# A one-layer hybrid decoder step: four weight halves and most parameters issued by GpSimd instead of SP and ACT

## Chip, cores and metric

One core of a Trainium2 chip runs the whole step in one launch. The metric is the device time of one execution in microseconds; the profile is of another execution, taken by the hardware profiler. Times in the rows count from the start of the profiled span.

## What is computed

1024 prompt tokens and 64 sample tokens (8 sequences of 8) go through one layer; everything is float32.

```
h    = rms_norm(x, norm_g)
proj = h @ w_in                       # (tokens, 1024) x (1024, 3088)
a, gl, zc, q, k, v, zg, lr = split(proj)
u    = a * sigmoid(gl)                # 512 channels
cv   = depthwise_causal_conv(u, width 31)
cv   = silu(group_layer_norm(cv)) @ w_pw + b_pw
cv   = cv * silu(zc)
gk   = log_sigmoid(lr @ w_alpha + b_alpha) / 16
o, S = gla_chunked(q, k, v, gk, S0)   # gated linear attention, 4 heads
o    = per_head_rms_norm(o) * gla_g * silu(zg)
y    = rms_norm(x + concat(cv, o) @ w_out, final_g)
```

The outputs are y, the last 30 rows of u and the states S, for prompt and samples apart. The parameters that are vectors (norm_g, conv_w, biases, and so on) come in one array `par` of 128 x 152; columns 0 to 7 hold norm_g, the last one the epsilon of the norms.

## The kernel before

Every float32 matmul operand is split in two float32r parts, hi and lo (ACT copies hi, VectorE subtracts to get lo), and three float32r matmuls stand for one float32 product: hi x hi, hi x lo and lo x hi. A weight tile of 128 output channels comes in two halves of 4 x 128 rows of w_in (256 KB each): `s_gl0_1` is the staged second half of tile 0 of gl, `h_gl0_1` and `l_gl0_1` its parts.

Tokens go in three blocks (`CHUNKS`): number 0 (0 to 383), number 1 (384 to 767) and number 2 (768 to 1087, with the samples). Number 2 is loaded and used first (`FIRST = 2`), and for the first four weight tiles (gl0, a0, gl1, a1) it is multiplied before its norm is known: `raw_split` scales x by norm_g alone (`hh`, `hl`), and the factor rs comes in afterwards. Blocks 0 and 1 are normed first: `rms_scale` squares the eight x tiles on ACT (`sq0_k`, `sq1_k`), adds them on VectorE, sums over channels on TensorE (`ms`) and takes Ln and Exp on ACT (`rs`); `rms_split` scales x on VectorE and splits it into `hh` and `hl`.

Operations are recorded in program order by `prog.add` with a cost, and `Program.schedule` then lists them: on each engine it takes, at the planner's own time, the ready operation with the lowest priority number. Loads on SP and ACT share one planned data path (`dma_end`); operations on POOL have a cost and a lag instead, and `o.bytes` does not count there. `prog.hold` adds a dependency for the planner. The engines then run their lists in order, and the framework puts in the semaphores that the data and the reused buffers need. Each of SP's loads also waits until the one eight places before it has landed. The buffers `wst` for staged weights are four (`NST`), and from `STAGE` on halves of the first tiles are staged in `big` buffers instead.

In the loading loop (L1047 to L1063) `par` is loaded by ACT, the first halves (`h == 0`) in two pieces each and the second halves (`h == 1`) in one, all by SP, between the x tiles of block 2.

Of the kernel before, what the change touches and what calls it, by code (L numbers as in the profile page):

```python
# [29 lines left out]
C_NG, C_BA, C_CW, C_CB, C_CG, C_CBT, C_BP, C_GG, C_EPS, NPAR = 0, 8, 10, 134, 138, 142, 146, 150, 151, 152  # L30
# [16 lines left out]
STATES_AT = 1  # L47
CN_LAST = 2
ADD_LAG = 5000
STICK = 60  # L50
SLACK = 500
SLACK_FROM = 45000
# [85 lines left out]
class Program:  # L138
# [51 lines left out]
    def schedule(self):  # L190
# [51 lines left out]
        while events:  # L242
# [18 lines left out]

            if same is not None and t > SLACK_FROM and same.prio < best.prio + STICK:
                best = same
# [72 lines left out]
def build(tc, A, O):  # L336
    nc = tc.nc
    ctx = ExitStack()
    V, S, G, T = nc.vector, nc.scalar, nc.gpsimd, nc.tensor
    prog = Program({"big": NBIG, "unit": NUNIT, "wst": NST, "wl": NW, "wh": NW, "ps": 8, "kT": 2, "S": 8, "ss": 9},  # L340
                   {"ps": 3, "unit": 8, "big": 2})
# [4 lines left out]
    def R(v):  # L346
        return v.ap() if isinstance(v, View) else v
# [50 lines left out]
    def dma(out, in_, late=False, eng="SP", small=False):  # L398
        v = out if isinstance(out, View) else in_
        if late:  # L400
            prog.hold = late
        q = nc.sync if eng == "SP" else S
        prog.add(eng, lambda: q.dma_start(R(out), R(in_)), [out], [in_], 0,  # L403
                 nbytes=v.n * 4 * (v.part[1] - v.part[0]) * (6 if small else 1))

    def dma_add(out, in_):

        prog.add("POOL", lambda: G.dma_start(R(out), R(in_), accum_op=ALU.add), [out], [in_], 1000,
                 nbytes=out.n * 4 * P, lag=ADD_LAG)

# [15 lines left out]
    with ctx:  # L426
# [9 lines left out]
        def VT(pool, tag, shape, dt, name):  # L436
            return View.of(Tile_(pool, tag, shape, dt, name))
# [14 lines left out]
        par = VT(fixed, "par", [P, NPAR], F32, "par")  # L452
# [36 lines left out]
        def x_load(c, ks=range(KT), late=False, eng="SP"):  # L489
            t0, n = CHUNKS[c]  # L490
            for k in ks:
                xk = rows("x", k, F32)[:, t0:t0 + n]
                dma(xk, A["xT"][:, k, t0:t0 + n], late, eng)
                xs[(c, k)] = xk
# [15 lines left out]
        def raw_split(ks):  # L510

            for k in ks:
                g, xk = pc(C_NG + k), xs[(FIRST, k)]
                hi, lo = part("hh", k, FIRST), part("hl", k, FIRST)
                act(hi, xk, AF.Copy, scale=g)
                stt(lo, xk, g, hi.bitcast(F32), ALU.mult, ALU.subtract)
                raw[k] = hi, lo

        def rms_scale(c):
            n = CHUNKS[c][1]  # L520
            ms = pt(f"ms{c}")[:, :n]
            g = SQ_SUM[c]
            for k in range(KT):
                sq = un(f"sq{c}_{k}")[:, :n]
                act(sq, xs[(c, k)], AF.Square)
                if k % g == 0:
                    acc = sq
                else:
                    tt(acc, acc, sq, ALU.add)
                if k % g == g - 1:  # L530
                    mm(ms, one_d, acc, k == g - 1, k == KT - 1)
            rs[c] = un(f"rs{c}")[:, :n]
            act(rs[c], ms, AF.Ln, bias=eps)
            act(rs[c], rs[c], AF.Exp, scale=-0.5)
# [11 lines left out]
        def load_split(name, src, k, m, stage=None):  # L546
            st = VT(stage or wst, "big" if stage else "wst", [P, k, m], F32, f"s_{name}")
            hi = VT(wh, "wh", [P, k, m], F32R, f"h_{name}")
            lo = VT(wl, "wl", [P, k, m], F32R, f"l_{name}")
            dma(st, src)  # L550
            split(hi, lo, st)
            return hi, lo
# [6 lines left out]
        def whalf_parts(kind, i, h, stage=None):  # L559

            name, src = f"{kind}{i}_{h}", A["w_in"][mt[(kind, i)]]
            st = VT(stage or wst, "big" if stage else "wst", [P, 4, P], F32, f"s_{name}")
            hi = VT(wh, "wh", [P, 4, P], F32R, f"h_{name}")
            lo = VT(wl, "wl", [P, 4, P], F32R, f"l_{name}")

            def piece(a, b, eng):
                dma(st[:, a:b, :], src[:, 4 * h + a:4 * h + b, :], eng=eng)
                split(hi[:, a:b, :], lo[:, a:b, :], st[:, a:b, :])

            return (hi, lo), piece  # L570
# [473 lines left out]
                mix_samples(4 + i, o[:, 256:n])  # L1044


        dma(par, A["par"], eng="ACT")  # L1047
        w0, w1 = [[], []], [[], []]
        for h in range(2):
            parts_ = []  # L1050
            for w, kind, ct in ((w0[0], "gl", 0), (w0[1], "a", 0), (w1[0], "gl", 1), (w1[1], "a", 1)):
                tiles, piece = whalf_parts(kind, ct, h, big if 4 * h + len(parts_) >= STAGE else None)
                w.append(tiles)
                parts_.append(piece)

            n = 2 if h == 0 else 4
            for j in range(0, 4, n):
                for i, piece in enumerate(parts_):
                    if i < n:
                        k = 4 * h + j + i  # L1060
                        x_load(FIRST, range(k, k + 1))
                        raw_split(range(k, k + 1))
                    piece(j, j + n, "SP")  # L1063
        rms_scale(FIRST)
        x_load(0)
        x_load(1, late=True)
# [450 lines left out]
```

## Time and profile before

| | us |
|---|---|
| median of 3 runs | 463.41 (463.18 to 463.77) |
| profiled execution | 463.69 |
| its span | 461.9 |
| TensorE busy in the span | 451.9 |
| VectorE busy | 393.1 |
| ACT busy | 306.6 |
| GpSimd busy | 19.1 |

The span is the time from the first to the last instruction that the profiler saw; the rest of the execution lies around it. Matmuls are pipelined, so the busy time of one (0.31 us for 320 columns) is longer than the distance to the next. DMA share is the mean busy share of the 16 DMA engines; a landing time is counted from the start of the issue.

### The profile page before, as it was taken

Reading aid. Unit: us, or ns where it says so; the run is one execution under the profiler, and the core shown is the slowest. Engines: PE = TensorE matmul, PEld = TensorE weight load, DVE = VectorE, ACT = ScalarE, POOL = GpSimd, SP = SyncE. Lnnn points to the kernel's source line nnn. Section 1 sums busy time; section 2 is a strip of 40 time slices with the busy share of each in tenths; the row PEclk is TensorE's granted clock in tenths of the full one; section 3 lists DMA queues with packets and bytes.
Section 4 is the critical chain, followed back from the end, with each engine's and each line's share of the span. In section 5 each row is a group of like instructions: output and inputs, shape, how many; then the busy total and the mean of one; then the engine's idle time right before and its main releaser. Section 6 shows DMA issues by size and latency. Waiting matters only on the chain.

```text
span 461.9 us, 7604 instructions
## 1 busy us (share of the span) xinstructions
PE 451.9 (98%) x2728; PEld 413.8 (90%) x2728; DVE 393.1 (85%) x629; ACT 306.6 (66%) x782; POOL 19.1 (4%) x38
## 2 busy tenths in 40 slices
PE   8899999999999999999999999999999999999994
PEld 8699989999888899898999899999999988888783
DVE  5789999999999999999999899953549847988684
ACT  7767979363643623658866797653899548879554
POOL 1000000000000000000000000000000023220000
PEclk9999999999999999999999999999999999999998
DMA  7935340141200040003211211011235474476744
GB/s 214 328 126 104 67 146 15 47 68 35 57 0 1 23 153 9 2 8 107 70 57 48 82 58 45 26 66 64 77 81 183 118 196 68 78 166 152 270 151 182
DMA packets 36485, 43.26 MB, mean 94 GB/s; under 512 B 13024, under 2 KB 21344, under 8 KB 36448
## 3 DMA queue, kind: packets, MB, share of 16 engines
q1 hardware_dynamic: 33856, 38.25, 26.5%
q0 software_dynamic: 2304, 4.20, 5.7%
q8 instruction: 21, 0.34, 0.3%
q10 hardware_dynamic: 288, 0.34, 0.2%
q14 instruction: 16, 0.13, 0.1%
HBM read 36.58 MB, written 6.19 MB: 93 GB/s over the span
## 4 chain that ended last, share of the span: by engine, by line
PE 91%; DMA 3%; ACT 2%; DVE 1%; SPq 1%; issue 1%
PE ya L415 11%; PE p_zc L415 10%; PE p_zg L415 10%; PE pv L415 10%; PE p_gl L415 9%; PE p_a L415 9%; PE p_k L415 5%; PE pw L415 5%; PE p_q L415 5%; PE yc L415 5%; PE po L415 2%; DMA x<-in_xT 2%; PE pys L415 2%; DMA s_a<-in_w_in 1%; SPq L403 1%; PE px L415 1%
## 5 line engine op out<-in xcount | busy, mean ns | idle before, releaser
L364 DVE SCALAR_TENSOR_TENSOR cv<-u,par,cv 128x1024 f32<-128x1024 f32 x120 | 150.9, 1278 | 0.2
L415 PE MATMUL p_gl<-hh,h_gl 128*128 128x384 f32 (+1 forms) x96 | 32.2, 336 | 2.0 <-ACT h_gl L358 1.3
L358 ACT ACTIVATE pr<-us,par 128x64 f32<-128x64 f32 x124 | 32.3, 343 | 0.0
L415 PE MATMUL p_gl<-hh,l_gl 128*128 128x384 f32 (+1 forms) x96 | 32.3, 336 | 0.0
L415 PE MATMUL p_gl<-hl,h_gl 128*128 128x384 f32 (+1 forms) x96 | 31.7, 331 | 0.2 <-DVE hl L364 0.2
L415 PE MATMUL p_zc<-hh,h_zc 128*128 128x384 f32 (+1 forms) x96 | 31.7, 330 | 0.0
L415 PE MATMUL p_a<-hl,h_a 128*128 128x384 f32 (+1 forms) x96 | 31.6, 329 | 0.0
L415 PE MATMUL p_zc<-hl,h_zc 128*128 128x384 f32 (+1 forms) x96 | 31.5, 328 | 0.0
L415 PE MATMUL p_zc<-hh,l_zc 128*128 128x384 f32 (+1 forms) x96 | 31.5, 328 | 0.0
L415 PE MATMUL p_zg<-hl,h_zg 128*128 128x384 f32 (+1 forms) x96 | 31.5, 328 | 0.0
L415 PE MATMUL p_zg<-hh,l_zg 128*128 128x384 f32 (+1 forms) x96 | 31.4, 327 | 0.0
L415 PE MATMUL p_zg<-hh,h_zg 128*128 128x384 f32 (+1 forms) x96 | 31.4, 327 | 0.0
L415 PE MATMUL p_a<-hh,h_a 128*128 128x384 f32 (+1 forms) x96 | 31.3, 326 | 0.0
L415 PE MATMUL p_a<-hh,l_a 128*128 128x384 f32 (+1 forms) x96 | 31.2, 326 | 0.0
L415 PE MATMUL pv<-h_v,hl 128*128 128x512 f32 x64 | 25.0, 390 | 0.0
L415 PE MATMUL pv<-l_v,hh 128*128 128x512 f32 x64 | 24.9, 390 | 0.0
L415 PE MATMUL pv<-h_v,hh 128*128 128x512 f32 x64 | 24.9, 389 | 0.0
L415 PEld LDWEIGHTS p_gl<-hh,h_gl 128*128 128x128 f32 x96 | 18.0, 188 | 3.6 <-ACT h_gl L358 2.1
L415 PEld LDWEIGHTS p_gl<-hh,l_gl 128*128 128x128 f32 x96 | 18.0, 188 | 1.3 <-DVE l_gl L368 0.4
L415 PEld LDWEIGHTS p_gl<-hl,h_gl 128*128 128x128 f32 x96 | 18.0, 188 | 0.7 <-DVE hl L364 0.4
L368 DVE TENSOR_TENSOR o<-o,zg 128x384 f32<-128x384 f32 (+1 forms) x12 | 6.2, 534 | 14.5 <-ACT zg L358 14.5
L415 PEld LDWEIGHTS p_zc<-hh,h_zc 128*128 128x128 f32 x96 | 18.1, 188 | 0.3 <-issue 0.2
(345 smaller groups left out, 1284.2 us busy)
## 6 DMA issues: line engine op xcount, KB each, us to landing
xr<-in_x SPq DMA_DIRECT2D x16, 256.0 KB, 4.8
out_y<-xr SPq DMA_DIRECT2D x15, 256.0 KB, 2.1
x<-in_xT SPq DMA_DIRECT2D x16, 192.0 KB, 5.3
T<-in_w_out POOLq DMA_DIRECT2D x12, 256.0 KB, 5.1
s_v<-in_wv SPq DMA_DIRECT2D x16, 128.0 KB, 2.8
s_zc<-in_w_in SPq DMA_DIRECT2D x8, 256.0 KB, 2.6
s_zg<-in_w_in SPq DMA_DIRECT2D x8, 256.0 KB, 2.6
s_gl<-in_w_in SPq DMA_DIRECT2D x6, 256.0 KB, 4.8
```

The lines of the kernel that those rows point to most:

```text
L358: return S.activation(R(out), R(in_), func, **kw)
L364: return prog.add("DVE", lambda: V.scalar_tensor_tensor(R(out), R(a), R(s), R(b), op0, op1), [out], [a, s, b], out.n / 0.96 + 67 + 62 * is ...
L368: return prog.add("DVE", lambda: V.tensor_tensor(R(out), R(a), R(b), op), [out], [a, b], out.n / 0.96 + 67)
L403: prog.add(eng, lambda: q.dma_start(R(out), R(in_)), [out], [in_], 0, nbytes=v.n * 4 * (v.part[1] - v.part[0]) * (6 if small else 1))
L415: o = prog.add("PE", lambda: T.matmul(R(ps), R(lhsT), R(rhs), start=start, stop=stop, skip_group_check=True), [ps], [lhsT, rhs], c / share ...
```

## The change

`dma` gets a third way of issuing: by GpSimd, with a planned cost of 1000 ns and a lag of 3500. The parameters are loaded in two pieces, columns 0 to 7 by ACT as before, the other 144 by GpSimd; the four second halves of the first four weight tiles go to GpSimd too. Each of the five is held, in the planner, behind the split of the second x tile.

```
+LOAD_LAG = 3500
@@ def dma
         q = nc.sync if eng == "SP" else S
+        if eng == "POOL":
+            prog.add(eng, lambda: G.dma_start(R(out), R(in_)), [out], [in_], 1000,
+                     nbytes=v.n * 4 * (v.part[1] - v.part[0]), lag=LOAD_LAG)
+            return
         prog.add(eng, lambda: q.dma_start(R(out), R(in_)), [out], [in_], 0,
@@ loading loop
-        dma(par, A["par"], eng="ACT")
+        dma(par[:, 0:C_BA], A["par"][:, 0:C_BA], eng="ACT")
...
                         x_load(FIRST, range(k, k + 1))
                         raw_split(range(k, k + 1))
-                    piece(j, j + n, "SP")
+                        if k == 1:
+                            started = prog.ops[-1]
+                            prog.hold = started
+                            dma(par[:, C_BA:], A["par"][:, C_BA:], eng="POOL")
+                    if h == 1:
+                        prog.hold = started
+                    piece(j, j + n, "POOL" if h == 1 else "SP")
```

The planner makes new lists for all engines. On SP before, from the fourth x tile of block 2 on; x4 to x7 of 128x320 are block 2, those of 128x384 block 0:

```order
L403 DMA x4_156<-in_xT 128x320
L403 DMA x5_167<-in_xT 128x320
L403 DMA x6_176<-in_xT 128x320
L403 DMA s_gl1_1_185<-in_w_in 128x512
L403 DMA x7_192<-in_xT 128x320
L403 DMA s_a1_1_201<-in_w_in 128x512
L403 DMA s_gl0_1_211<-in_w_in 128x512
L403 DMA x0_88<-in_xT 128x384
L403 DMA x1_98<-in_xT 128x384
L403 DMA s_a0_1_234<-in_w_in 128x512
```

And GpSimd's list with the change, from the last of its first memsets:

```order
L394 MEMSET vs_103 64x512
L405 DMA par_86<-in_par 128x144
L405 DMA s_gl1_1_168<-in_w_in 128x512
L405 DMA s_a1_1_191<-in_w_in 128x512
L405 DMA s_gl0_1_212<-in_w_in 128x512
L405 DMA s_a0_1_231<-in_w_in 128x512
L394 MEMSET u1_323 128x30
```

The four second halves have left SP's list, where x4 to x7 and the tiles of block 0 now follow each other, and stand on GpSimd behind the rest of the parameters.

ACT's list before, from the last squares of block 0 (`sq0_k`) to the first split of block 0 (`hh` of 128x384); `sq1_k` are the squares of block 1, `rs0` is the factor of block 0:

```order
L358 ACTIVATE sq0_7_363<-x7_192 128x384
L358 ACTIVATE rs0_380<-ms0_338,par_86 128x384
L358 ACTIVATE rs0_380<-rs0_380 128x384
L358 ACTIVATE sq1_0_390<-x0_88 128x384
L358 ACTIVATE sq1_1_397<-x1_98 128x384
L358 ACTIVATE hh0_114<-x0_88 128x384
L358 ACTIVATE sq1_2_407<-x2_116 128x384
L358 ACTIVATE hh1_130<-x1_98 128x384
L358 ACTIVATE hh2_172<-x2_116 128x384
L358 ACTIVATE sq1_3_423<-x3_127 128x384
```

The same place with the change:

```order
L359 ACTIVATE sq0_7_360<-x7_189 128x384
L359 ACTIVATE sq1_0_366<-x0_88 128x384
L359 ACTIVATE sq1_1_372<-x1_98 128x384
L359 ACTIVATE sq1_2_378<-x2_116 128x384
L359 ACTIVATE rs0_382<-ms0_344,par_86 128x384
L359 ACTIVATE sq1_3_389<-x3_129 128x384
L359 ACTIVATE rs0_382<-rs0_382 128x384
L359 ACTIVATE sq1_4_401<-x4_161 128x384
L359 ACTIVATE sq1_5_407<-x5_173 128x384
L359 ACTIVATE sq1_6_413<-x6_180 128x384
L359 ACTIVATE sq1_7_418<-x7_189 128x384
L359 ACTIVATE hh0_113<-x0_88 128x384
```

Two squares of block 1 stood ahead of the first split of block 0; now all eight do, three of them ahead of `rs0` as well.

TensorE's list before, at the end of block 2 (`p_a1_2`) and the start of block 0 (`p_gl0_0`):

```order
L415 MATMUL p_a1_2_196<-hh6_248,l_a1_1_293 128x320
L415 MATMUL p_a1_2_196<-hh7_264,h_a1_1_277 128x320
L415 MATMUL p_a1_2_196<-hl7_279,h_a1_1_277 128x320
L415 MATMUL p_a1_2_196<-hh7_264,l_a1_1_293 128x320
L415 MATMUL p_gl0_0_410<-hh0_114,h_gl0_0_125 128x384
```

And with the change, where `ms1` is the sum over channels of block 1's first squares:

```order
L420 MATMUL p_a1_2_205<-hh5_244,l_a1_1_293 128x320
L420 MATMUL ms1_415<-sq1_0_366,one_d_100 128x384
L420 MATMUL p_a1_2_205<-hh6_251,h_a1_1_284 128x320
L420 MATMUL p_a1_2_205<-hl6_263,h_a1_1_284 128x320
L420 MATMUL p_a1_2_205<-hh6_251,l_a1_1_293 128x320
L420 MATMUL p_a1_2_205<-hh7_259,h_a1_1_284 128x320
L420 MATMUL p_a1_2_205<-hl7_272,h_a1_1_284 128x320
L420 MATMUL p_a1_2_205<-hh7_259,l_a1_1_293 128x320
L420 MATMUL p_gl0_0_431<-hh0_113,h_gl0_0_124 128x384
```

The first of the two sums of block 1 has moved from inside block 0 to the last seven matmuls of block 2.

## Rows read from the trace of the kernel before

**Rows 1.** The page: busy us, share and count by engine; tenths in 40 slices.

```profile
PE 451.9 (98%) x2728; PEld 413.8 (90%) x2728; DVE 393.1 (85%) x629; ACT 306.6 (66%) x782; POOL 19.1 (4%) x38
...
PE   8899999999999999999999999999999999999994
...
```

**Rows 2.** TensorE's waits: for whom, us in total, times, longest us.

```profile
...
PE p_gl L415 <- ACT h_gl L358: 1.3, 2, 0.9
...
PE p_gl L415 <- ACT hh L358: 0.6, 2, 0.4
...
```

**Rows 3.** Stretches: length; busy PE, PEld, DVE, ACT, POOL; clock; DMA share; GB/s.

```profile
...
0.00:5.00 5.00, 3.89 (x19) 3.71 (x19) 0.77 (x3) 2.51 (x4) 1.97 (x11) 1.00 0.54 152
5.00:10.00 5.00, 4.63 (x27) 4.01 (x28) 4.29 (x11) 4.39 (x12) 0.00 (x0) 1.00 0.89 262
10.00:15.00 5.00, 4.07 (x26) 3.55 (x26) 4.03 (x10) 3.79 (x9) 0.00 (x0) 1.00 0.87 273
15.00:20.00 5.00, 4.56 (x26) 3.83 (x27) 4.48 (x9) 4.69 (x11) 0.00 (x0) 1.00 1.00 347
20.00:25.00 5.00, 5.00 (x26) 3.74 (x25) 1.78 (x4) 3.08 (x7) 0.00 (x0) 1.00 1.03 364
...
```

**Rows 4.** TensorE's timeline, 12 to 38 us: start, duration, instruction, idle before.

```profile
...
14.11 0.41 PE L415 MATMUL p_gl<-hh,h_gl 128*128 128x320 f32 x1 [0.90 <-ACT h_gl L358]
...
26.56 0.44 PE L415 MATMUL p_gl<-hh,h_gl 128*128 128x384 f32 x1 [0.40 <-ACT hh L358]
...
35.87 1.45 PE L415 MATMUL ms<-sq,one_d 128*128 128x384 f32 x4
...
37.34 0.34 PE L415 MATMUL p_gl<-hl,h_gl 128*128 128x384 f32 x1
...
```

**Rows 5.** ACT's timeline, 25 to 31 us.

```profile
...
25.01 1.09 ACT L358 ACTIVATE sq<-x 128x384 f32<-128x384 f32 x2 [0.30 <-DMA x<-in_xT]
26.00 0.51 ACT L358 ACTIVATE hh<-x 128x384 fp32r<-128x384 f32 x1
...
28.49 1.75 ACT L358 ACTIVATE sq<-x 128x384 f32<-128x384 f32 x4
30.14 1.34 ACT L358 ACTIVATE hh<-x 128x384 fp32r<-128x384 f32 x3
...
```

**Rows 6.** Tile x, 20.5 to 20.6 us: block 1's third load (the later of the two).

```profile
...
L403 SPq DMA_DIRECT2D x<-in_xT x2: 422/426/430, 20.1 to 20.6; - x2
...
DMA to landing us min/median/max: 5.4/5.4/5.4
```

**Rows 7.** Tile x, 24.4 to 24.6 us: block 1's last load.

```profile
...
L403 SPq DMA_DIRECT2D x<-in_xT x1: 328/328/328, 24.5 to 24.5; - x1
...
DMA to landing us min/median/max: 3.9/3.9/3.9
```

**Rows 8.** All engines' timeline, 0 to 6 us: TensorE's warm-up, ACT's first split.

```profile
...
1.07 3.86 PE L415 MATMUL warm<-warm 128*128 128x128 f32 x18 [1.07 <-DVE warm L475]
...
3.69 0.56 ACT L358 ACTIVATE hh<-x,par 128x320 fp32r<-128x320 f32 x1 [1.66 <-DMA par<-in_par]
...
```

**Rows 9.** Tile x, 0 to 30 us: landing of all its 24 loads.

```profile
...
DMA to landing us min/median/max: 2.7/4.4/6.4
```

**Rows 10.** GpSimd's timeline: its first part's end, and DMAs in a row.

```profile
...
1.86 0.52 POOL L393 MEMSET vs<- 64x512 f32 x1
...
386.41 3.53 POOL L408 DMA_DIRECT2D T<-in_w_out  x4 [7.18 <-ACT T L358]
...
```

**Rows 11.** Tile T, the whole span: landing of the loads issued for it.

```profile
...
DMA to landing us min/median/max: 2.9/4.5/7.8
```

**Rows 12.** SP's waits between 4 and 25 us.

```profile
...
SPq L403 <- DMA s_gl<-in_w_in: 1.9, 3, 1.0
SPq L403 <- DMA s_a<-in_w_in: 1.9, 4, 0.8
...
SPq L403 <- DVE l_a L368: 0.5, 1, 0.5
...
```

## Prediction

> **What bounds the kernel now.** The page comes first: TensorE is busy for 451.9 of 461.9 us, and all its slices from the third to the last but one show 9 [rows 1], so a delay of the loading phase goes through to the end one for one. Next is the list of TensorE's waits: two for ACT's h_gl (1.3 us) and two for ACT's hh (0.6 us) [rows 2]. The table of stretches shows what is scarce before 25 us, where these lie: the 16 DMA engines, with a share of 0.54 up to 5 us, then 0.89, 0.87, 1.00 and 1.03 [rows 3].
>
> TensorE comes to block 0 at 26.56 us, after a wait for ACT's hh [rows 4]. That hh, at 26.00, stands in ACT's list behind two squares of block 1, which began at 25.01, when the first of block 1's loads had landed [rows 5]. So two of block 1's eight loads already decide when block 0 starts. The third was issued at 20.6 and landed 5.4 us later, at 26.0 [rows 6]; the last, issued at 24.5, landed 3.9 us later, at 28.4 [rows 7].
>
> **The change, part by part.**
>
> *Parameters.* ACT's first hh waited for the parameters until 3.69 us [rows 8]. A load of 4 KB instead of 76 KB may land earlier, but the x load beside it, issued at the same time (0.75), needs at least 2.7 us [rows 9], so at most 0.2 us is won on ACT. On TensorE nothing is: its warm-up matmuls run from 1.07 for 3.86 us, to 4.93 [rows 8]. I take 0; the other columns are first read much later, for rs.
>
> *Five DMAs on GpSimd.* They stand behind the memset of vs, which ends at 2.38 us [rows 10]. The hold orders them in the planner's list only: in the built program the parameters and two weight halves (gl1, a1) have no wait, and the last two wait until VectorE has split the tiles whose buffers they take. Four GpSimd DMAs in a row took 3.53 us, 0.88 each [rows 10], so the first three are issued by 2.38 + 3 x 0.88 = 5.0 us, and the last two some time after 9. GpSimd's next work is memsets of u and lr_w, for which nobody near waits: cost 0. Landing took 2.9 to 7.8 us for its loads, which also accumulate [rows 11]. Four issues leave SP's list, worth something only where the DMA engines have room.
>
> *Removed stalls.* With the halves there early, TensorE's waits for h_gl (0.90 us at 14.11, 1.3 in all) can go [rows 2, 4]. What is late next is decided by the new order, and this is the term that counts.
>
> *ACT's new order.* All eight squares of block 1 and both rs of block 0 now stand ahead of block 0's first hh. After the third load has landed, ACT has square 2, Ln, square 3, Exp and squares 4 to 7 to do: eight instructions. Four squares took 30.14 - 28.49 = 1.65 us, so 0.41 each [rows 5]; Ln and Exp of this width are taken at the same. With landings as before, hh starts at 26.0 + 8 x 0.41 = 29.3 us; the last landing (28.4, plus one square, 28.8) is covered by that. TensorE began 0.56 us after hh did (26.00 to 26.56) [rows 4, 5], so now at 29.9 instead of 26.56: +3.3 us. VectorE's part, scaling x by rs, is not later: rs is out at 26.0 + 4 x 0.41 = 27.6.
>
> *Given back.* One sum over block 1's squares (ms1) now stands ahead of block 0 on TensorE; in before both stood inside block 0. The two cost 37.34 - 35.87 = 1.47 us less the one 384-column matmul between them, some 0.17 at full clock, so 1.30 [rows 4]; 0.65 us is done while TensorE would wait anyway. Sum: 3.3 - 0.65 = +2.65 us. The 1.3 us of removed stalls lie inside the longer wait and buy nothing.
>
> *When block 1 lands* is the open size. The same bytes must come before it (parameters, two blocks of x, twelve weight halves), so if the DMA engines carry them at the old pace the landings stay. If the second queue fills what stood idle, 0.11 + 0.13 of two 5 us stretches (1.2 us) and about 0.5 us of the first [rows 3], they come at most 1.7 us earlier, and the sum falls to +0.95. On the other side, two weight halves now run ahead of block 2's last x tile, where one did: 256 KB more, 1.0 us at 262 GB/s [rows 3]. ACT's work after that tile, up to the last split on VectorE, moves by as much, and SP's last s_a load, which already waited 0.5 us for that split [rows 12], holds block 1's loads behind it. But those took 5.4 us to land [rows 6] where an undisturbed one takes 2.7 [rows 9], so some 2.7 us of late issue is backlog and costs nothing. So the landing may move by -1.7 to +1.0. I take 0: SP waited 3.8 us for landings of s_gl and s_a alone [rows 12], each of its loads standing until the one eight places before has landed, so the engines had work queued while they moved 262 to 273 GB/s, and another queue brings them no more.
>
> Here the table of stretches, read by its share, would let the second queue win: the engines are not full before 15 us [rows 3]. The Trainium skill ("DMA: Bandwidth & Descriptors", "Issuing engines are not separate DMA queues") speaks against the change: DMAs run on the same 16 engines whichever engine starts them, and starting them from several saves only the time of issuing. By that rule the landings stay and the sum is +2.65; by the idle share it is +0.95.
>
> The profiled execution took 463.69 us, 1.79 more than its span and 0.28 more than the median of the runs, 463.41. So a profile of the change would give 466.3 and the median 466.1.
>
> **Rivals.**
>
> *The second queue fills the engines.* Landings 1.0 to 1.7 us earlier give +0.95 to +1.65: 464.4 to 465.1. For it: shares 0.89 and 0.87 [rows 3]. Against: SP stood still for landings at that time [rows 12].
>
> *Faster: the early loads run at the later pace.* The first 15 us moved 5 x (152 + 262 + 273) = 3.43 MB; later 347 to 364 GB/s were moved [rows 3]. From about 2 us on at that pace they take 9.9 to 9.4 us and are there by 11.9 to 11.4, so all that follows comes 3.1 to 3.6 us earlier: 2.65 - 3.1 to 2.65 - 3.6, that is -0.45 to -0.95, 463.0 to 462.5. It decides from the point where block 1's third load lands before 23.3 us (26.0 - 2.65). For it: the later pace came with rows of 1.5 and 2 KB, and two GpSimd loads bring 2 KB rows into a stretch of 1 and 1.25 KB. Against: those short rows stay the larger part.
>
> *Slower still: GpSimd's loads crowd out the first pieces.* If they take every second turn, block 2's last x comes 2 to 3 us later; SP's s_a loads then wait for their splits beyond the 2.7 us of backlog, and block 1 slips by up to 1.0: +3.65, 467.1. For it: the share is already 0.89 there.
>
> *It doesn't do what it says:* GpSimd's loads land so late (7.8 us) [rows 11] that TensorE waits for h_gl longer than 0.90 us. It would still meet the same wait at block 0, so the time is the forecast's, 466.1.
>
> **How the numbers follow.** The forecast, with the last rival that gives its time, gets 0.59, crowding 0.18, the filled engines 0.13, the later pace 0.10. The forecast's own range is 465.2 to 466.8. The range of 8 in 10 runs from 464.0, between the filled engines and the later pace, to 467.3, beyond crowding. A change of less than 0.2%, 0.93 us, can't be told from none here. Above 464.34 lie the forecast, crowding and nearly all of the filled engines, 0.9 in all; a tenth of it goes to no change for mechanisms further on that swallow a late start: slower 0.80. Below 462.48 lies the far end of the later pace and what goes beyond it: 0.07. The rest, 0.13, is no change.
>
> **What would show it.** Right: TensorE's first 384-column p_gl at about 29.9 us, with its wait put down to ACT's hh; eight squares ahead of that hh; the last x of block 1 landing within 0.5 us of 28.4; GpSimd's DMAs at about 2.4, 3.3 and 4.1 us and two after 9; no wait for h_gl over 0.5 us; from 31 us on the same work at the same pace. Wrong: a block 0 that starts before 27.2 us, or a third load that lands before 25. If the start is late and the time is not, a wait further on has swallowed it.

## The result, and the profile after

The changed kernel takes 466.90 us (median of 4 runs, 466.33 to 468.48), the kernel before 463.59 beside it (4 runs, 463.18 to 464.01). By the medians that is 3.3 us slower. The ratio, worked out from all the runs and not from the medians, is 1.0083, with an interval of 1.0069 to 1.0096: slower by 3.2 to 4.5 us. The forecast was 466.1, with a range of its own from 465.2 to 466.8 and one of 8 in 10 up to 467.3. The direction was right; the loss was larger than forecast, 0.1 us beyond the forecast's own range. The profiled execution took 466.85 us, its span is 465.1.

The page of the changed kernel, where [rows 1] stand for before:

```profile
...
PE 452.3 (97%) x2728; PEld 414.8 (89%) x2728; DVE 392.7 (84%) x629; ACT 307.0 (66%) x782; POOL 22.0 (5%) x43
...
PE   6899999999999999999999999999999999999994
...
```

TensorE does the same work (452.3 against 451.9 us) in a span that is 3.2 us longer. Of the slices only the first shows less (6 in place of 8), but a slice is 11.6 us and its digit is coarse: by the stretches below TensorE is busy for 0.5 us less up to 10 us and for 2.5 us less up to 25, so the loss builds up over the whole loading phase. Its waits, which answer [rows 2]:

```profile
...
PE p_gl L420 <- ACT h_gl L359: 3.4, 3, 2.6
PE ms L420 <- DVE sq L369: 1.5, 3, 1.0
...
```

The waits for h_gl, which the change was to shorten, grew from 1.3 to 3.4 us. The stretches [rows 3]:

```profile
...
0.00:5.00 5.00, 3.93 (x19) 3.93 (x19) 1.14 (x3) 2.87 (x5) 3.53 (x12) 1.00 0.60 154
5.00:10.00 5.00, 4.09 (x20) 3.40 (x18) 1.72 (x4) 1.43 (x5) 0.00 (x0) 1.00 0.94 292
10.00:15.00 5.00, 3.08 (x20) 3.02 (x21) 4.18 (x11) 4.63 (x13) 1.25 (x4) 1.00 0.83 253
15.00:20.00 5.00, 4.13 (x27) 3.61 (x26) 4.71 (x10) 3.95 (x9) 0.00 (x0) 1.00 0.98 322
20.00:25.00 5.00, 4.43 (x20) 2.88 (x19) 2.65 (x6) 4.40 (x10) 0.00 (x0) 1.00 0.78 262
...
```

In the first 10 us a little more is moved (154 and 292 GB/s against 152 and 262), but ACT is busy for 1.43 us of the second stretch, where it was for 4.39: the bytes that come are not those that it needs. From 20 to 25 us the DMA engines run at 0.78, where they were full (1.03).

TensorE's timeline, to compare with [rows 4]:

```profile
...
11.92 0.42 PE L420 MATMUL p_gl<-hh,h_gl 128*128 128x320 f32 x1 [2.63 <-ACT h_gl L359]
...
29.50 0.91 PE L420 MATMUL ms<-sq,one_d 128*128 128x384 f32 x2 [0.97 <-DVE sq L369]
...
31.14 0.44 PE L420 MATMUL p_gl<-hh,h_gl 128*128 128x384 f32 x1
...
```

Block 0 (the first p_gl with 384 columns) starts at 31.14 us, 4.58 later than before; the forecast said 29.9, with a wait for ACT's hh. The wait that is seen, 0.97 us at 29.50, is another: it is for `ms`, the sum over block 1's squares, which the new list puts ahead of the last matmuls of block 2. The hh would have held TensorE as long: it starts at 30.57, and 0.56 us behind that, as in before, is 31.13. ACT's timeline ahead of it [rows 5]:

```profile
...
9.86 0.42 ACT L359 ACTIVATE h_a<-s_a 128x256 fp32r<-128x256 f32 x1 [1.94 <-DMA s_a<-in_w_in]
...
20.20 0.63 ACT L359 ACTIVATE h_a<-s_a 128x512 fp32r<-128x512 f32 x1 [0.51 <-DMA s_a<-in_w_in]
...
25.55 0.52 ACT L359 ACTIVATE sq<-x 128x384 f32<-128x384 f32 x1 [0.92 <-DMA x<-in_xT]
26.40 1.03 ACT L359 ACTIVATE sq<-x 128x384 f32<-128x384 f32 x2 [0.32 <-DMA x<-in_xT]
...
28.06 0.52 ACT L359 ACTIVATE sq<-x 128x384 f32<-128x384 f32 x1 [0.15 <-DMA x<-in_xT]
...
28.90 1.77 ACT L359 ACTIVATE sq<-x 128x384 f32<-128x384 f32 x4
30.57 1.75 ACT L359 ACTIVATE hh<-x 128x384 fp32r<-128x384 f32 x4
...
```

The new order is there as forecast, eight squares ahead of the first hh. But hh comes at 30.57 and not at 29.3, since block 1's tiles land later: three of the squares wait for a load. Where that begins is shown by the DMA queues between 5 and 9 us (packets, MB, share of the 16 engines), first before, then after; q1 is SP's queue, q0 GpSimd's:

```profile
...
DMA packets 1072, 1.05 MB, mean 263 GB/s; under 512 B 120, under 2 KB 1072, under 8 KB 1072
...
q1 hardware_dynamic: 1072, 1.05, 89.8%
...
```

```profile
...
DMA packets 742, 1.09 MB, mean 272 GB/s; under 512 B 98, under 2 KB 620, under 8 KB 742
...
q1 hardware_dynamic: 582, 0.59, 48.6%
q0 software_dynamic: 160, 0.50, 42.8%
...
```

The engines moved 1.05 and 1.09 MB, so the second queue brought next to nothing; it took nearly half. SP's queue, with all the pieces that TensorE needs first, got 0.59 MB in place of 1.05. The load of x that SP issued at 3.55 us in both kernels (tile x, 3.5 to 3.6 us; before, then after):

```profile
...
DMA to landing us min/median/max: 3.9/3.9/3.9
```

```profile
...
DMA to landing us min/median/max: 7.1/7.1/7.1
```

So this tile lands 3.2 us later. GpSimd's timeline shows what follows:

```profile
...
2.34 0.70 POOL L405 DMA_DIRECT2D par<-in_par  x1
3.03 0.57 POOL L405 DMA_DIRECT2D s_gl<-in_w_in  x1
3.58 0.54 POOL L405 DMA_DIRECT2D s_a<-in_w_in  x1
12.82 0.54 POOL L405 DMA_DIRECT2D s_gl<-in_w_in  x1 [8.70 <-DVE l_gl L369]
14.02 0.54 POOL L405 DMA_DIRECT2D s_a<-in_w_in  x1 [0.66 <-DVE l_a L369]
...
```

The last two halves wait for splits that are late with the first pieces. They land 5.4 and 6.2 us after their issue, the second at 20.2, where ACT waits for it. SP's timeline around its loads of the next weights and of block 1, before and after, and its wait for that half's split:

```profile
...
18.28 1.31 SPq L403 DMA_DIRECT2D s_a<-in_w_in  x2
19.64 5.18 SPq L403 DMA_DIRECT2D x<-in_xT  x8
```

```profile
...
19.67 2.25 SPq L408 DMA_DIRECT2D s_a<-in_w_in  x2
21.96 2.25 SPq L408 DMA_DIRECT2D x<-in_xT  x3
```

```profile
...
SPq L408 <- DVE l_a L369: 1.4, 1, 1.4
...
```

SP's second s_a load takes the buffer of that late half and waits 1.4 us for its split, and block 1's loads stand behind it: they begin 2.32 us later. Block 1's third load is issued at 23.8 (20.6 before) and lands after 3.0 us in place of 5.4 [rows 6]: 0.8 us later in all. Its last load is issued at 26.2 (24.5 before) and lands after 3.9 us as before [rows 7], at 30.1 in place of 28.4. The third and the last (the later of the two in either answer):

```profile
...
L408 SPq DMA_DIRECT2D x<-in_xT x2: 432/868/1304, 22.4 to 23.8; - x2
...
DMA to landing us min/median/max: 3.0/3.5/3.9
```

```profile
...
L408 SPq DMA_DIRECT2D x<-in_xT x2: 430/430/431, 25.7 to 26.2; - x2
...
DMA to landing us min/median/max: 3.9/3.9/3.9
```

### The profile page after: what moved, and what is told of

Read it like the earlier page. It is cut to its first block, busy times and chain, and to the rows that moved or that the text cites. A ratio compares the mean times of both kernels' runs of the same rounds, so it can differ in the third digit from the quotient of the medians.

```text
span 465.1 us, 7626 instructions
## 1 busy us (share of the span) xinstructions
PE 452.3 (97%) x2728; PEld 414.8 (89%) x2728; DVE 392.7 (84%) x629; ACT 307.0 (66%) x782; POOL 22.0 (5%) x43
## 4 chain that ended last, share of the span: by engine, by line
PE 92%; DMA 4%; ACT 1%; DVE 1%; SPq 1%; issue 1%; DVEq 0%
PE ya L420 11%; PE p_zc L420 10%; PE p_zg L420 10%; PE pv L420 10%; PE p_a L420 9%; PE p_gl L420 9%; PE p_q L420 5%; PE p_k L420 5%; PE pw L420 5%; PE yc L420 5%; DMA x<-in_xT 2%; PE po L420 2%; PE pys L420 2%; DMA s_a<-in_w_in 1%; PE pa L420 1%; PE px L420 1%
## 5 line engine op out<-in xcount | busy, mean ns | idle before, releaser
L420 PE MATMUL p_a<-hh,h_a 128*128 128x384 f32 (+1 forms) x96 | 32.3, 337 | 0.3 <-ACT h_a L359 0.3
L420 PEld LDWEIGHTS p_a<-hh,h_a 128*128 128x128 f32 x96 | 18.2, 189 | 0.9 <-ACT h_a L359 0.5
L420 PEld LDWEIGHTS p_a<-hl,h_a 128*128 128x128 f32 x96 | 18.1, 188 | 0.4
```

Source lines behind the costliest of these rows:

```text
L420: o = prog.add("PE", lambda: T.matmul(R(ps), R(lhsT), R(rhs), start=start, stop=stop, skip_group_check=True), [ps], [lhsT, rhs], c / share ...
```

## The experiments

Besides the times, the start of TensorE's 301st matmul is given, counted in the trace (58.00 us in before): in before and in the changed kernel TensorE has no wait behind it, and all kernels have the same 2728 matmuls. It is the same piece of work in all but two of them, where this is said. In the changed kernel it comes 4.03 us later; the last matmul 3.39 later, without a wait between the two. A trace is one execution, which can lie some way from the median of the runs. New lists for one engine also move what the planner puts on the others, so no experiment changes one thing alone.

**ACT's order alone.** The order is set by dependencies in the planner's list.

```diff
+        rs_op[0][0].deps.add(sq_op[(1, 2)])
+        sq_op[(1, 3)].deps.add(rs_op[0][0])
...
+        hh_op[(0, 0)].deps.add(sq_op[(1, 7)])
```

> The loads stay as before (all by SP, the parameters whole); only ACT's list is the changed one: the eight squares of block 1 and both rs of block 0 ahead of block 0's first hh. Theory A, ACT's order is the cost (the prediction's step): hh starts at about 29.3 us, block 0 on TensorE at 29.9, +2.65 us. Theory B, the loads are the cost (the first pieces land late behind GpSimd's halves, and the order only follows them): with the old loads nothing is late but the hh, and less than 1 us is lost. Theory C, both stand side by side and either is enough: +2 to +2.7 us, like A; it parts from A in the next kernel.

Measured: 466.69 us (5 runs), before 463.48; ratio 1.0081, 1.0069 to 1.0093. ACT's and TensorE's timelines:

```profile
...
27.78 1.75 ACT L358 ACTIVATE sq<-x 128x384 f32<-128x384 f32 x4
29.43 1.75 ACT L358 ACTIVATE hh<-x 128x384 fp32r<-128x384 f32 x4
```

```profile
...
29.99 0.45 PE L415 MATMUL p_gl<-hh,h_gl 128*128 128x384 f32 x1
```

hh at 29.43 and block 0 at 29.99, where the forecast had 29.3 and 29.9. A and C hold, B falls: the order alone is enough. By the times it costs 3.2 us, as much as the whole change, though the loads land as before. The trace shows why it is more than the 2.65 of the sum. Block 0 starts 3.43 us late, and right behind its start another us is lost, which the changed kernel does not lose: VectorE's first hl of block 0 comes behind four scalings of x in this kernel's list (29.03 to 31.23; two in the changed one), and TensorE gets to it only 1.13 us after its matmul of gl or a before that:

```profile
...
30.89 0.65 PE L415 MATMUL pl<-x,lr_w 128*32 128x272 f32 x2
31.75 0.45 PE L415 MATMUL p_gl<-hl,h_gl 128*128 128x384 f32 x1 [0.21 <-DVE hl L368]
...
```

The planner filled such gaps with six small matmuls for lr_w (`pl`), which come at 64 us in before. So the piece of work that is the 301st matmul elsewhere is the 307th here, at 61.81 us: 3.81 late.

**The loads alone.** The changed loads, with before's order on ACT forced in the same way.

> The loads are the changed ones (second halves and most parameters by GpSimd), ACT's list around block 0 is the old one (two squares of block 1 ahead of the first hh). Theory A, ACT's order alone: within 0.5 us of before. Theory B, the loads alone: the whole +3.3 us. Theory C, either is enough: TensorE stalls for h_gl early on (2.6 us at about 9 to 12 us, as in the changed kernel), ends block 2 some 3 us later than before, and the time is +2.3 to +3.3 us although hh stands early in ACT's list.

Measured: 466.14 us (6 runs, 464.49 to 467.25); ratio 1.0060, 1.0045 to 1.0074. TensorE's waits, the start of block 0, and its clock (length, busy PE, clock, DMA share, GB/s):

```profile
...
PE p_gl L420 <- ACT h_gl L359: 2.2, 1, 2.2
...
```

```profile
...
28.85 0.34 PE L420 MATMUL p_gl<-hh,h_gl 128*128 128x384 f32 x1
```

```profile
...
12.00:13.00 1.00, 1.00 (x6) 0.50 0.97 293
13.00:14.00 1.00, 1.00 (x5) 0.50 0.93 299
...
```

TensorE comes to block 0 without a wait for hh, which is early, and still 2.3 us late: block 2 itself ends late. The 301st matmul is 2.40 us late. A falls, C holds: the late first pieces and the order on ACT stand side by side, and by the times either alone costs most of the loss. But part of the 2.40 is the clock, which fell to 0.50 after the stall: the matmuls of 320 columns start 0.27 us apart from 11.64 to 14.57 us and 0.15 apart behind, so these eleven steps cost some 1.3 us (an estimate). Without it about 1.1 would be left. The times agree with that: the fastest of the six runs is 1.0 us above before, and the two slowest are those with the lowest granted clock (0.989 over the whole run, 0.994 and 0.996 in the others).

**The parameters alone.** All weight halves back on SP.

```diff
-                    piece(j, j + n, "POOL" if h == 1 else "SP")
+                    piece(j, j + n, "SP")
```

> Only the parameters are split (first 8 columns by ACT's queue, 144 columns by GpSimd); the weight halves stay on SP, and ACT's list near block 0 is the old one. Theories A and B both: nothing, within 0.3 us of before. If the many small packets of the parameters' second part are what holds up SP's first pieces, it is slower by over 1 us.

Measured: 464.06 us (11 runs); ratio 1.0012, 1.0002 to 1.0022. TensorE's 301st matmul is 0.46 us earlier, the last 0.14 later; between them no wait was found, only another order of matmuls. No part of the early loss comes from the parameters; by the medians the kernel is 0.6 us slower, a little more than the 0.3 that was allowed for.

**hh ahead of the squares.** Before's loads, and a dependency of block 1's first square on block 0's fourth hh.

> The loads stay as before; the first four hh of block 0 stand ahead of all squares of block 1 in ACT's list, so that block 0 waits for none of block 1's loads. Theory A and C: TensorE's wait of 0.40 us ahead of block 0 goes, and with the squares out of the way up to 1 us is won: -0.4 to -1.0 us. Rival: the sums over block 1's squares (ms1) come later on TensorE and rs of block 1 with them, and the wait moves there: 0.

Measured: 463.04 us against 463.48 (11 and 23 runs); ratio 0.9992, 0.9984 to 1.0001. Block 0 starts at 25.14 us, 1.4 earlier than before, with no wait ahead of it:

```profile
...
24.53 1.59 ACT L358 ACTIVATE hh<-x 128x384 fp32r<-128x384 f32 x3 [0.69 <-DVE x L364]
27.53 1.06 ACT L358 ACTIVATE hh<-x 128x384 fp32r<-128x384 f32 x2 [1.41 <-DVE x L364]
...
```

In the profile, which is of the fastest of the 11 runs, the last matmul comes 1.17 us earlier. The medians differ by 0.44 us, which the interval can't tell from nothing. It is the only version here whose median is below both kernels.

**Smaller pieces by GpSimd.** Old order on ACT, as in the next three.

```diff
-            prog.add(eng, lambda: G.dma_start(R(out), R(in_)), [out], [in_], 1000,
...
+            for a_, b_ in (((0, n_), (n_, 2 * n_)) if n_ else ((None, None),)):
+                d_, s_ = (out[:, a_:b_, :], in_[:, a_:b_, :]) if n_ else (out, in_)
+                prog.add(eng, lambda d_=d_, s_=s_: G.dma_start(R(d_), R(s_)), [d_], [s_], 1000,
```

> As the kernel with only the loads changed (old order on ACT), but each of GpSimd's four weight halves goes in two DMAs of half the row, so that its packets are smaller than 4096 bytes; bytes, queue and place stay. Theory P, the size of GpSimd's packets takes the turns of the 16 DMA engines from SP's packets of 1024 and 1280 bytes: TensorE's stall for h_gl at 9 to 12 us shrinks from 2.2 us to 1.2 us or less, and of the 2.4 to 2.7 us lost at most 1.3 is left. Theory Q, the bytes alone do it, since 512 KB run ahead of the first pieces whatever their packets: the stall stays at about 2.2 us and the loss at 2.4 to 2.7 us.

Measured: 464.41 us (11 runs); ratio 1.0021, 1.0013 to 1.0030; a stall of 1.2 us. The times are those of theory P, but the edit did not do what it was for: up to 28 us the trace has 256 packets of 4096 bytes on GpSimd's queue in either kernel, for rows of 1 KB as for those of 2 KB. What changed is the pace: the first halves are issued in four pieces with the parameters between them (2.3 to 4.6 us), the planner also put SP's last s_a load behind block 1, and from 5 to 9 us q0 moved 0.43 MB:

```profile
...
q1 hardware_dynamic: 637, 0.64, 59.2%
q0 software_dynamic: 162, 0.43, 29.9%
...
```

So this says nothing on the size of packets.

**The early halves, the late halves.**

```diff
+                    piece(j, j + n, "POOL" if h == 1 and i >= 2 else "SP")
```

> Only the two halves that wait for nothing (gl and a of the second tile, issued by GpSimd at 3.0 to 3.6 us) stay on GpSimd; the other two go back to SP; old order on ACT. Theories P and Q: the whole early stall, +2.4 us or a little more. Rival R, it is the two late halves, issued at 12.8 and 14.0 us, that delay block 1: less than +0.8 us here.

> Only the two halves that wait for a buffer (gl and a of the first tile) are issued by GpSimd; the two early ones go back to SP; old order on ACT. Theories P and Q: no early stall beyond the old 0.9 us, within 0.5 us of before. Rival R: +1.5 us or more.

Measured: early halves only, 465.71 us (6 runs, 464.64 to 466.45), ratio 1.0046, 1.0034 to 1.0059; a stall of 2.5 us, the 301st matmul 1.03 us late with the clock at 1.00. That trace is of one of the faster runs (464.78); the two slowest (466.4) are again those with the lowest granted clock, 0.989. Late halves only, 464.12 us (12 runs), ratio 1.0015, 1.0006 to 1.0023: 0.8 us slower, somewhat more than the 0.5 expected and not far from the parameters alone, which are in it; 301st matmul 0.45 late. So the early halves are most of the cost of the loads, and R falls. But SP's timeline shows that block 1's delay needs both (loads alone, early only, late only):

```profile
...
21.56 3.41 SPq L408 DMA_DIRECT2D x<-in_xT  x6
...
```

```profile
...
19.76 4.77 SPq L408 DMA_DIRECT2D x<-in_xT  x8
```

```profile
...
19.60 4.44 SPq L408 DMA_DIRECT2D x<-in_xT  x8
```

With only one pair on GpSimd block 1's loads start as before (19.64). Only when GpSimd's late halves stand behind splits that its early ones have delayed are they 2 us late.

**A later start.** GpSimd's loads wait, in the built program, for the split of block 2's fourth x tile, or of its second, the one that the change's hold names.

```diff
+            if o.real is not None:
+                after(i, o.real.name)
```

> The loads as changed, the old order on ACT, but GpSimd's loads (the parameters' second part, and by it all behind it) wait in the built program until ACT and VectorE have split block 2's fourth x tile, at about 11 us. Theories P and Q, first pieces crowded out: the stall at 9 to 12 us is gone and most of the 2.4 us with it, unless the halves now land too late: between -0.5 and +1.0 us. If GpSimd's issue as such (its queue, its descriptors) costs the time, it stays at +2 us or more.

> The loads as changed, the old order on ACT, and the hold of the planner's list made a wait of the built program: GpSimd's loads start once block 2's second x tile is split (about 7 us). Theories P and Q: the first pieces are past by then, the later ones (landing at 9 to 13 us) are crowded in their place: a stall of 0.5 to 1.5 us and +0.5 to +1.5 us. Were the early start harmless, the time would be that of the kernel with only the loads changed (+2.7 us) or more.

Measured: fourth tile, 464.14 us (11 runs), ratio 1.0016, 1.0008 to 1.0025. The stall at 9 us is gone. Another of 2.2 us comes at 13 us, for the sum over block 2's squares, which the planner now puts ahead of the matmuls with the halves; these land only at 17 us and later. The time is inside the expectation. Second tile, 465.88 us (9 runs, 464.35 to 467.68), ratio 1.0043, 1.0028 to 1.0057: 2.5 us, worse than expected. The first two halves are issued at 6.8 and 7.3 us, the stall becomes 3.6 us, and in the trace, which is of the slowest run, the clock falls behind it:

```profile
...
15.00:20.00 5.00, 2.99 (x10) 0.57 1.00 354
...
```

Making the hold real at the place it names would not have saved the change.

**The same bytes by ACT's queue.** Every list of the first 40 us as with the early halves only; the two are issued by ACT behind the first hh.

```diff
+                    piece(j, j + n, "ACT" if h == 1 and i >= 2 else "SP")
```

> As the kernel with only the two early halves on GpSimd, every list of the first 40 us the same, but these two halves are issued by ACT's queue right behind the first hh (about 4 us), so that their bytes come about when GpSimd's did (its first packets began at 5.1 us) in packets of 2048 bytes in place of 4096. Theory P, the size of the packets decides who gets the engines: the stall for h_gl at 9 to 12 us is clearly shorter than 2.5 us (1.2 us or less) and the time at most +1.2 us. Theory Q, the bytes decide: the stall stays at 2 us or more, and the time at about +2.1 us.

Measured: 469.71 us (4 runs), ratio 1.0129, 1.0109 to 1.0149. Most of that is not about the question: in the trace the 221st matmul, taken here since the order is another further on, is 1.95 us late (1.06 with the early halves on GpSimd). The rest comes behind 45 us, where the forced lists end and the planner ordered matmuls otherwise. TensorE waited 2.4 us for h_gl in the first 60 us. The queues from 6 to 10 us, the four in which the halves came (q10 is ACT's):

```profile
...
q1 hardware_dynamic: 695, 0.69, 53.1%
q10 hardware_dynamic: 278, 0.51, 37.4%
...
```

Packets of 2048 bytes took 0.51 of 1.19 MB, those of 4096 by GpSimd 0.50 of 1.09. So by the queues P falls: half the packet size leaves a second queue nearly the same share (0.43 and 0.46 of the bytes), and the engine that issues makes no great difference. By the stalls the run decides nothing. The 2.4 us are three waits, 1.18 at 6 us, 0.28 at 11 and 0.95 at 18, and not the one of 2 us at 9 to 12 that Q asked for; and the first has another cause, since the second issue kept ACT idle for 1.7 us ahead of its first h_gl. That also speaks against ACT as a place for it.

**Parameters split and hh first.**

> Only the parameters split (second part by GpSimd), all weight halves on SP, and the first four hh of block 0 ahead of block 1's squares on ACT. The parts alone gave TensorE's block 0 a start 0.5 us (parameters) and 1.1 us (order) earlier in the profiles, and the medians +0.6 and -0.4 us. If the gains of the early part add up and reach the end: -0.8 to -1.5 us. If what the split of the parameters lost at about 200 us stays: -0.2 to +0.4 us.

Measured: 463.48 us against 463.39 (11 and 20 runs), ratio 0.9998, 0.9988 to 1.0008. The 301st matmul is only 0.33 us early, the last 0.05: the gains did not add up.

## Why the forecast was right in sign and too small

*Parameters: 0.* Nearly: alone +0.6 us by the medians (interval 0.1 to 1.0), none of it early.

*Five DMAs on GpSimd.* Right: issued at 2.3, 3.0 and 3.6 us, without a wait, and two after 9. One took 0.54 to 0.70 us, not 0.88, so they came a little earlier than priced.

*Removed stalls.* Wrong: the expectation of no wait for h_gl over 0.5 us met one of 2.63. The halves that the forecast saw early did come early, at the price of the first pieces of all others. The sum had them at nothing because the later wait covers them, and that hid the error there: the loads alone cost 2.40 us by the 301st matmul, of which some 1.3 are the clock.

*ACT's new order: +3.3 at the start of block 0.* Right: 3.43 when tried alone, with hh and block 0 within 0.13 us.

*Given back: 0.65.* About right: in the changed kernel 4.58 at the start of block 0 had become 4.03 by the 301st matmul, 0.55 less.

*When block 1 lands: "I take 0".* This is the step that failed. Measured: the third load 0.8 us later and the last 1.6, where the bounds were -1.7 to +1.0; hh 1.14 us later than with the order alone (30.57 against 29.43), and block 0 1.15 (31.14 against 29.99). The terms are then 3.43 + 1.15 - 0.55, the 4.03 of the 301st matmul. Another 0.64 came back later without a wait, which no term of the sum foresaw: 3.39 by the last matmul, and the span grew by 3.2. Without that piece of luck the forecast would have missed by about 1.4 us in place of 0.8. The size of 1.15 is read from two traces at one place; the times do not show it, since the order alone lost about as much behind that place, on VectorE's list.

The working let the splits slip by 1.0 us, as 256 KB more at 262 GB/s, and set 2.7 us of backlog against it. The backlog was there (the third load's landing fell from 5.4 to 3.0 us), but block 1's loads began 2.3 us late and the third was issued 3.2 us late. A queue that shares the engines delayed the other one by more than one load, and GpSimd's late halves added their own wait and landing of 6.2 us. SP's gate, named in that step, was the place.

*The rivals.* Crowding (0.18, 467.1) comes nearest, in time and in mechanism, but not by the tile that it named. Block 2's last x lands only 0.2 us later (issued at 11.0 and landed after 3.0 us, against 8.6 and 5.2), not 2 to 3; late were the pieces ahead of it, the third x by 3.2 us, and then GpSimd's own late halves, for whose split SP waited. Filled engines and the later pace fall by one row: 263 GB/s before, 272 after, from 5 to 9 us; over the first 15 us 3.43 MB became 3.50. That is also what the Trainium skill says ("DMA: Bandwidth & Descriptors", "Issuing engines are not separate DMA queues"): starting DMAs from several engines saves issue time alone. The same page of the Trainium skill ("Queues, rings and completion order") says that each DMA engine takes turns between the queues that have work; the trace agrees in that a second queue got 42.8% of the engines' time beside 48.6%, and 0.46 of the bytes (0.50 of 1.09 MB). The forecast used the first rule for the sum of the bytes and did not ask whose bytes they are.

## What to carry to other kernels

Here a second DMA queue added little pace while the engines had work (263 to 272 GB/s) and took nearly half of it away from the queue that held the urgent pieces. So it is a place for loads that are as urgent, or for loads that start when the urgent ones have landed; that either would win was not shown, and every version here with weight halves in a second queue was slower than before, by 0.8 us at least. When a load is moved, ask not only whether the sum of bytes comes as early, but which pieces come later, and follow them to the next instruction that queues behind their buffers. And when a planner's list changes with the loads, price the list and the loads apart, then together: here the list alone cost 3.2 us by the medians, the loads alone 2.7, and both 3.3. Count the same piece of work when two traces are compared: the 301st matmul of a list in another order is another matmul.

## What the runs showed that was not expected

TensorE's clock did not answer a stall in the same way each time. In the changed kernel it stood still from 9.3 to 11.9 us and with the early halves only for 2.5 us, and the granted clock stayed at 1.00 (2.4 GHz). With the loads alone a stall of 2.2 us in the same place was followed by 0.50 (1.2 GHz) from 12 to 14 us, one of 2.2 us in the run that waits for the fourth tile by 0.50 from 16 to 19, and after 3.6 us of waiting the mean from 15 to 20 us was 0.57. What decides was not tried. It goes with the spread of such kernels: with the loads alone, with the early halves only and with the wait for the second tile, the slowest runs are those with the lowest granted clock (0.989).

GpSimd's loads of rows of 1 KB and of 2 KB both went in packets of 4096 bytes, where SP's rows of 1 KB went in packets of 1024.
